# Input transfers of the first layer become tasks of their own, and TensorE multiplies zeros at the start

## The chip, the cores and the metric

One core of a Trainium2 chip runs the whole program. The metric is device time in microseconds (us) of one execution, the median of several runs. A core has five engines that run their own instruction queues in order and wait for each other by semaphores: TensorE (PE; its weight loads are listed as PEld), VectorE (DVE), ScalarE (ACT), GpSimd (POOL) and SyncE (SP). In this kernel SP issues almost every transfer from HBM.

## The reference, cut to what matters

Two layers of a hybrid encoder, 256 tokens of width 2048. Per layer:

```python
h = rms_norm(x, norm_g)
u = h @ w_in                       # 2048 x 15944, cut into q, k, v, z, gates of four branches
mkv = mem @ w_mem_kv               # 256 memory tokens, 2048 x 1024: keys and values of branch M
y = [sparse attention, retention, gated recurrence, attention on mkv]
merged = sum(sigmoid(gate[n]) * ((y[n] * silu(z[n])) @ w_branch[n]) for n in range(4))
x = x + merged @ w_out
```

`mem` doesn't depend on the layers, so the memory keys and values of both layers can be computed first.

## The kernel before, in words

Every large product is done with split operands: a weight tile `raw` in float32 is cast by ACT to `whi` (line 231), DVE subtracts to get `wlo` (line 232), and TensorE adds three matmuls: `whi` by the high part of the activations (line 257), `wlo` by the high part (258) and `whi` by the low part (259).

Weights come in **slabs** of 512 rows of the contraction, 1 MB at the usual 512 columns. A slab is cut into two **half slabs** of 256 rows, each with one `whi` and one `wlo` tile and 12 matmuls of 512 columns. `plan` lists the slabs in order: 16 for the memory keys and values (`mk`, `mv`; two layers, two products, four slabs each), then those of the layers (`u`, `bw`, `wo`). There are four `raw` buffers, and four buffers each for `whi` and `wlo`, so ACT and DVE can be at most four half slabs ahead of TensorE. A load into a `raw` buffer is issued by `split_weights` right behind the second cut of the oldest slab, and SP waits for DVE to be done with that buffer.

Side work is written as Python generators. `stream.add` makes one a **task**. After each half slab's matmuls `gemms` calls `stream.pump()`, which counts a tick and lets at most two tasks take a step, and then `split_weights()`. So a step's instructions stand, on each engine, between the cuts of two half slabs. A bare `yield` in a task passes to a later tick; `stream.rest(n)` blocks it for n ticks. Nothing is reordered behind this: what an engine meets in its queue is what was written first.

`constants()` (line 640) is one task. It loads a first block of constants (`csb`), `qks`, `ngs` and `lbs`, then four blocks of the transposed input (`xr`, from `xt`), each followed two yields later by `split_scaled` (lines 282 and 283), which cuts `xr` into `x0bh` and `x0bl`. Then four blocks of `x` into `xs`, each followed two yields later by two squares on ACT (line 661), then the scale `rs`, the rest of the constants, and masks on POOL. While it is the first task in the list it takes a step at each tick. Its result is asked for behind the memory products, by `stream.finish(start)`.

`fold` transposes a tile by 32x32 blocks: one DVE transpose and 16 small transfers, on POOL and SP in turn (line 308). The memory keys of layer 0 pass through one (`mk0pt`), and ACT scales the result (line 360).

Of the kernel before, what the change touches and what calls it, by code (L numbers as in the profile page):

```python
# [13 lines left out]
AF = mybir.ActivationFunctionType  # L14
# [69 lines left out]
BLOCKED = object()  # L84
# [2 lines left out]
    ((0, 0), (0, 1), (0, 2), (0, 3), (1, 0), (1, 1), (1, 2), (1, 3)),  # L87
)
GEN, HL, RAW = 18, 4, 4
MOVES, STEPS, BANKS = 4, 2, 2  # L90


class Stream:
# [79 lines left out]
def trunk(ctx: ExitStack, tc: tile.TileContext, x, xt, memt, ng, qkg, hg, lbl, win, wmem, wbr, wout,  # L173
          cf, out):
    nc = tc.nc
    te, ve, ac, po, sy = nc.tensor, nc.vector, nc.scalar, nc.gpsimd, nc.sync
# [4 lines left out]
    xtp = ctx.enter_context(tc.tile_pool(name="xtp", bufs=8))  # L181
# [4 lines left out]
    def G(shape, name, dt=F32):  # L186
        return gen.tile(shape, dt, tag="g", name=name)

    def SM(n, name):
        return sml.tile([128, n], F32, tag="s", name=name)  # L190

    def PB(name):
        return psb.tile([128, 1024], F32, tag="pb", name=name)

    def dram(t, off, pitch, n):
        return bass.AP(tensor=t.tensor, offset=t.offset + off, ap=[[pitch, 128], [1, n]])

    xs = cst.tile([128, 2, DM], F32, name="xs")
    csb = cst.tile([128, C_END], F32, name="csb")
    msb = cst.tile([128, len(LEVELS) * 512], U8, name="msb")  # L200
    ngs = cst.tile([128, L, 16], F32, name="ngs")
# [8 lines left out]
    stream = Stream()  # L210

    def load(fine=False):
        src, off, n = plan[stream.loaded]
        raw = wpool.tile([128, 4, n], F32, tag="raw", name="raw", bufs=RAW)
        stream.loaded += 1
        stream.raw.append((raw, n))

        def part(a, b):
            sy.dma_start(raw[:, a:b, :].rearrange("p k n -> p (k n)"), dram(src, off + a * n, 4 * n, (b - a) * n))
        if fine:  # L220
            return part
        part(0, 4)

    def split_weights(fine=False):
        raw, n = stream.raw[0]
        j = stream.cut % 2
        hi = wpool.tile([128, 2, n], F32R, tag="hi", name="whi")
        lo = wpool.tile([128, 2, n], F32R, tag="lo", name="wlo")
        for a, b in [(0, 1), (1, 2)] if fine else [(0, 2)]:
            r = raw[:, 2 * j + a:2 * j + b, :]  # L230
            ac.copy(hi[:, a:b, :], r)  # L231
            ve.tensor_sub(lo[:, a:b, :], r, hi[:, a:b, :].bitcast(F32))  # L232
        stream.parts.append((hi, lo))
        stream.cut += 1
        if j:
            stream.raw.popleft()
            if stream.loaded < len(plan):
                load()
# [32 lines left out]
    def split(src, pool, tag, name):  # L271
        hi = pool.tile([128, 4, 256], F32R, tag=tag, name=name + "h")
        lo = pool.tile([128, 4, 256], F32R, tag=tag, name=name + "l")
        ac.copy(hi, src)
        ve.tensor_sub(lo, src, hi.bitcast(F32))
        return hi, lo

    def split_scaled(src, g, pool, tag, name):
        hi = pool.tile([128, 4, 256], F32R, tag=tag, name=name + "h")
        lo = pool.tile([128, 4, 256], F32R, tag=tag, name=name + "l")  # L280
        for k in range(4):
            ac.activation(hi[:, k, :], src[:, k, :], AF.Copy, scale=g[:, k:k + 1])
            ve.scalar_tensor_tensor(lo[:, k, :], src[:, k, :], g[:, k:k + 1], hi.bitcast(F32)[:, k, :],
                                    op0=OP.mult, op1=OP.subtract)
        return hi, lo

    def rsq(ss, n, scale, name):
        v = SM(n, name + "v")
        ve.tensor_scalar(v, ss, scale, EPS, op0=OP.mult, op1=OP.add)
        r = SM(n, name + "r")  # L290
        po.tensor_tensor(r, v, nhalf.to_broadcast([128, n]), op=OP.pow)
        return r
# [309 lines left out]
    def split_pieces(hi, lo, raw, cuts):  # L602
        for k0, k1 in cuts:
            ac.copy(hi[:, k0:k1, :], raw[:, k0:k1, :])
            ve.tensor_sub(lo[:, k0:k1, :], raw[:, k0:k1, :], hi[:, k0:k1, :].bitcast(F32))

    def split_later(raw, after, name):
        yield from stream.rest(after)
        return split(raw, gen, "g", name)

    part = load(True)
    part(0, 1)
    raw = G([128, 4, 256], "memr")
# [10 lines left out]
        sy.dma_start(memr[b], memt[:, 4 * b:4 * b + 4, :])  # L624
    hi = G([128, 4, 256], "memh", F32R)
    lo = G([128, 4, 256], "meml", F32R)
    split_pieces(hi, lo, raw, [(0, 1), (1, 2)])
    split_weights(True)
    split_pieces(hi, lo, raw, [(2, 4)])
    split_weights(True)  # L630
    split_weights()
    split_weights()
# [4 lines left out]
    def keep(key, steps):  # L637
        box[key] = yield from steps

    def constants():  # L640
        sy.dma_start(csb[:, :C_D], cf[:, :C_D])
        sy.dma_start(qks, qkg)
        yield
        sy.dma_start(ngs, ng)
        sy.dma_start(lbs, lbl)
        yield
        xh = []
        for b in range(4):
            raw = G([128, 4, 256], "xr")
            sy.dma_start(raw, xt[:, 4 * b:4 * b + 4, :])  # L650
            yield
            yield
            xh.append(split_scaled(raw, ngs[:, 0, 4 * b:4 * b + 4], xtp, "xt", f"x0{b}"))
        ssq = SM(8, "ssq0")
        for c in range(4):
            sy.dma_start(xs[:, :, c * 512:c * 512 + 512], x[:, :, c * 512:c * 512 + 512])
            yield
            yield
            for t in range(2):
                sq = G([128, 512], "xsq")  # L660
                ac.activation(sq, xs[:, t, c * 512:c * 512 + 512], AF.Square,
                              accum_out=ssq[:, t * 4 + c:t * 4 + c + 1])
        rs = rms(ssq, 0)
        sy.dma_start(csb[:, C_D:], cf[:, C_D:])
        for i in range(len(LEVELS)):
            po.tensor_copy(msb[:, 512 * i:512 * i + 512].rearrange("p (g t) -> p g t", g=8),
                           csb[:, C_LEV + 64 * i:C_LEV + 64 * i + 64][:, None, :].to_broadcast([128, 8, 64]))
        lower_bounds()
        return xh, rs

    lbv = cst.tile([128, L, NH], F32, name="lbv")
    olb = cst.tile([128, L, NH], F32, name="olb")
# [1 line left out]
    def lower_bounds():  # L674
        mx, e, sm = SM(4, "lbm"), SM(8, "lbe").rearrange("p (l h) -> p l h", l=2), SM(4, "lbsum")
        ve.tensor_max(mx, lbs[:, 0, :], lbs[:, 1, :])
        for l in range(L):
            ve.tensor_sub(e[:, l, :], lbs[:, l, :], mx)
        ac.activation(e, e, AF.Exp)
        ve.tensor_add(sm, e[:, 0, :], e[:, 1, :])  # L680
        ve.reciprocal(sm, sm)
        for l in range(L):
            ve.tensor_mul(e[:, l, :], e[:, l, :], sm)
        ve.tensor_sub(lbv[:, 0, :], e[:, 0, :], e[:, 0, :])
        ve.tensor_add(sm, e[:, 0, :], e[:, 1, :])
        ve.tensor_sub(lbv[:, 1, :], sm, e[:, 0, :])
        ve.tensor_scalar(olb, lbv, -1.0, 1.0, op0=OP.mult, op1=OP.add)

    def rms(ssq, l):
        s2 = SM(2, f"ss{l}")  # L690
        ve.reduce_sum(s2, ssq.rearrange("p (t c) -> p t c", t=2), axis=AX.X)
        return rsq(s2, 2, 1.0 / DM, f"rs{l}")

    start = stream.add(constants())
    for l in range(L):
        def keys_of(ps, l=l):
            stream.add(keep(f"mk{l}", normed_t(ps, None, qks[:, l, 3:4], f"mk{l}")))

        def values_of(ps, l=l):
# [1 line left out]

        gemms(memx, [(wmem, (2 * l + i) * DM * 512) for i in range(2)], 512, ["mk", "mv"], order=MEM_ORDER[l],
              then=[keys_of, values_of])
    xh, rs = stream.finish(start)

    for l in range(L):
        sy.dma_start(hgs.rearrange("p a b -> p (a b)"), hg[l].partition_broadcast(128))
# [22 lines left out]
        if isinstance(rs, Task):  # L730
            rs = stream.finish(rs)
# [67 lines left out]
                ac.activation(sq, xc[:, t, :], AF.Square, accum_out=nssq[:, t * 4 + c:t * 4 + c + 1])  # L799
            return r  # L800

        def scale_of(nssq, ready):
            while not all(t.done for t in ready):
                yield BLOCKED
            return rms(nssq, 1)

        if l + 1 < L:
            nssq = SM(8, "ssq1")
        nx = []
# [7 lines left out]
            if l + 1 < L:  # L817
                nx.append(stream.add(turned(c, xs[:, :, c * 512:c * 512 + 512], nssq)))
        if l + 1 < L:
            xh, rs = nx, stream.add(scale_of(nssq, list(nx)))  # L820


def _cols(w, chunks):
# [41 lines left out]
```

## Time and profile before

| | us |
|---|---|
| median of 3 runs | 1905.28 (1904.95 to 1905.65) |
| the profiled execution, its own time | 1905.74 |
| span of the profiled execution, first to last instruction | 1903.9 |
| TensorE busy | 1885.3 |
| TensorE's waits on other engines, all named ones | 14.1 |
| mean granted TensorE clock | 0.997 |

The span is what the trace shows; the execution's own time is 1.8 us longer. In rows of the timeline the columns are: start in us from the span's start, length in us, engine, line, operation, output<-input, sizes, count, and in brackets the idle time ahead of it and what ended that. The length of a matmul is modelled and overlaps the next; their rate is read from start to start. In rows of waits: engine, tile and line that waited, what for, us in total, times, the longest. In rows of windows: busy time and instruction count of each engine in a stretch, then the granted TensorE clock, the busy share of the 16 DMA engines and GB/s.

### The profile page before, as it was taken

What the parts mean: (1) busy time and instruction counts of PE and PEld (TensorE: products, weight loads), DVE (VectorE), ACT (ScalarE), POOL (GpSimd) and SP (SyncE); (2) the same over time, 40 slices, a digit from 0 to 9 for tenths busy, and PEclk for the clock granted to TensorE, in tenths of its full rate; (3) what the DMA queues carried; (4) which work ended last, traced back from release to release, by engine and by line L of the source; (5) the groups of instructions that cost most, each with busy time, mean ns of one, the idle gap of its engine ahead of it and who ended that gap; (6) DMA issues with size and microseconds to landing.
All of it is one profiled execution on the core that took longest, in us unless ns stands there. A gap on an engine that the chain in (4) does not pass through costs nothing.

```text
span 1903.9 us, 23024 instructions
## 1 busy us (share of the span) xinstructions
PE 1885.3 (99%) x8736; PEld 1574.5 (83%) x8736; DVE 1127.7 (59%) x1204; ACT 863.5 (45%) x995; POOL 238.7 (13%) x377
## 2 busy tenths in 40 slices
PE   7999999999999999999999999999999999999999
PEld 6788988888888888888888898888888888888887
DVE  5455667776655555455565576767565555555554
ACT  5554345544444444444454435554444444444442
POOL 0211041222200000000000104122220000000000
PEclk9999999999999999999999999999999999999999
DMA  8765566668656565565565557666775656556553
GB/s 311 237 226 178 184 184 197 210 199 206 199 197 210 192 196 199 199 203 186 202 189 214 169 176 209 192 215 187 212 199 199 200 190 208 199 185 204 197 203 107
DMA packets 155502, 379.21 MB, mean 199 GB/s; under 512 B 102528, under 2 KB 103424, under 8 KB 114432
## 3 DMA queue, kind: packets, MB, share of 16 engines
q1 hardware_dynamic: 144128, 366.84, 59.2%
q0 software_dynamic: 11264, 10.90, 2.7%
q8 instruction: 69, 1.13, 0.3%
q14 instruction: 41, 0.34, 0.1%
HBM read 353.82 MB, written 2.10 MB: 187 GB/s over the span
## 4 chain that ended last, share of the span: by engine, by line
PE 94%; DVE 0%; issue 0%; DVEq 0%
PE u L257 24%; PE u L258 24%; PE u L259 24%; PE wo L258 3%; PE wo L259 3%; PE bw L258 3%; PE bw L259 3%; PE bw L257 3%; PE wo L257 3%; PE cl L575 1%; PE mov L439 0%; PE mlg L409 0%; PE ixrp L474 0%; PE aov L439 0%; PE alg L409 0%; PE cdg L562 0%
## 5 line engine op out<-in xcount | busy, mean ns | idle before, releaser
L232 DVE TENSOR_TENSOR wlo<-raw,whi 128x1024 fp32r<-128x1024 f32 (+2 forms) x674 | 802.3, 1197 | 657.7 <-ACT whi L231 657.3
L231 ACT CAST whi<-raw 128x1024 fp32r<-128x1024 f32 (+2 forms) x674 | 693.5, 1033 | 917.6 <-PE u L259 721.8
L308 POOL DMA_DIRECT2D mgp<-mgpi x48 | 27.6, 582 | 588.7 <-ACT whi L231 293.3
L257 PE MATMUL u<-whi,x12h 128*128 128x512 f32 (+2 forms) x256 | 99.0, 387 | 0.0
L257 PE MATMUL u<-whi,x02h 128*128 128x512 f32 (+2 forms) x256 | 99.0, 387 | 0.0
L257 PE MATMUL u<-whi,x11h 128*128 128x512 f32 (+2 forms) x256 | 98.9, 386 | 0.0
L257 PE MATMUL u<-whi,x13h 128*128 128x512 f32 (+2 forms) x256 | 98.9, 386 | 0.0
L257 PE MATMUL u<-whi,x03h 128*128 128x512 f32 (+2 forms) x256 | 98.9, 386 | 0.0
L257 PE MATMUL u<-whi,x01h 128*128 128x512 f32 (+2 forms) x256 | 98.8, 386 | 0.0
L257 PE MATMUL u<-whi,x00h 128*128 128x512 f32 (+2 forms) x256 | 98.4, 384 | 0.0
L257 PE MATMUL u<-whi,x10h 128*128 128x512 f32 (+2 forms) x256 | 98.4, 384 | 0.0
L258 PE MATMUL u<-wlo,x02h 128*128 128x512 f32 (+2 forms) x256 | 98.2, 383 | 0.0
L258 PE MATMUL u<-wlo,x12h 128*128 128x512 f32 (+2 forms) x256 | 98.2, 383 | 0.0
L258 PE MATMUL u<-wlo,x11h 128*128 128x512 f32 (+2 forms) x256 | 98.2, 383 | 0.0
L259 PE MATMUL u<-whi,x11l 128*128 128x512 f32 (+2 forms) x256 | 98.2, 383 | 0.0
L258 PE MATMUL u<-wlo,x03h 128*128 128x512 f32 (+2 forms) x256 | 98.2, 383 | 0.0
L258 PE MATMUL u<-wlo,x13h 128*128 128x512 f32 (+2 forms) x256 | 98.2, 383 | 0.0
L259 PE MATMUL u<-whi,x12l 128*128 128x512 f32 (+2 forms) x256 | 98.2, 383 | 0.0
L259 PE MATMUL u<-whi,x02l 128*128 128x512 f32 (+2 forms) x256 | 98.2, 383 | 0.0
L258 PE MATMUL u<-wlo,x01h 128*128 128x512 f32 (+2 forms) x256 | 98.2, 383 | 0.0
L259 PE MATMUL u<-whi,x01l 128*128 128x512 f32 (+2 forms) x256 | 98.1, 383 | 0.0
L259 PE MATMUL u<-whi,x10l 128*128 128x512 f32 (+2 forms) x256 | 98.1, 383 | 0.0
(370 smaller groups left out, 3706.8 us busy)
## 6 DMA issues: line engine op xcount, KB each, us to landing
raw<-in_win SPq DMA_DIRECT2D x240, 1024.0 KB, 4.9
raw<-in_wbr SPq DMA_DIRECT2D x32, 1024.0 KB, 4.8
raw<-in_wout SPq DMA_DIRECT2D x32, 1024.0 KB, 4.8
raw<-in_wmem SPq DMA_DIRECT2D x15, 1024.0 KB, 7.5
raw<-in_win SPq DMA_DIRECT2D x8, 656.0 KB, 4.2
raw<-in_win SPq DMA_DIRECT2D x8, 512.0 KB, 3.6
xr<-in_xt SPq DMA_DIRECT2D x4, 512.0 KB, 7.5
xs<-in_x SPq DMA_DIRECT2D x4, 512.0 KB, 6.2
```

Of the source, the lines that this page charges most:

```text
L231: ac.copy(hi[:, a:b, :], r)
L232: ve.tensor_sub(lo[:, a:b, :], r, hi[:, a:b, :].bitcast(F32))
L257: te.matmul(ps[:, t, :n], ah[:, 2 * j + k, c], wh[:, k, :], start=first, stop=False)
L258: te.matmul(ps[:, t, :n], ah[:, 2 * j + k, c], wl[:, k, :], start=False, stop=False)
L259: te.matmul(ps[:, t, :n], al[:, 2 * j + k, c], wh[:, k, :], start=False, stop=last)
L308: q.dma_start(whole[b, :, a], inner[a, :, b])
L575: te.matmul(ps[:, g * 64:g * 64 + 64].rearrange("p (b j) -> p b j", j=m), kd[:, g // 2, c], qd[:, g // 2, c].rearrange("p (b two j) -> p b ...
```

## The change

The task `constants()` is split into several. `first_constants` loads the small tiles; `first_turned(b)`, four tasks, issues its `xr` block at tick 3 + 4b and cuts it seven ticks later; `first_squares(c)`, four tasks, issues its block of `x` at tick 19 + 2c and squares it seven ticks later; `last_constants` issues the rest of the constants at tick 27 and uses them seven ticks later. `xh` and `rs` are now tasks that the first product of layer 0 asks for, instead of `stream.finish(start)`.

At the program's head DVE sets a tile `warm` to zero and TensorE does five float32 matmuls of 256 columns on it, into a PSUM tile `heat` that nothing reads. And the first two cuts of the memory input (`split_pieces`) now stand behind the first cut of the weights, instead of ahead of it.

```diff
-MOVES, STEPS, BANKS = 4, 2, 2
+MOVES, STEPS, BANKS, WARM = 4, 2, 2, 5
...
-    def split_weights(fine=False):
+    def split_weights(fine=False, then=None):
...
             ve.tensor_sub(lo[:, a:b, :], r, hi[:, a:b, :].bitcast(F32))
+            if then and a == 0:
+                then()
...
+    warm = G([128, 256], "warm")
+    ve.memset(warm, 0.0)
+    heat = PB("heat")
+    for i in range(WARM):
+        te.matmul(heat[:, :256], warm[:, :128], warm, start=True, stop=True)
     part = load(True)
...
-    split_pieces(hi, lo, raw, [(0, 1), (1, 2)])
-    split_weights(True)
+    split_weights(True, lambda: split_pieces(hi, lo, raw, [(0, 1), (1, 2)]))
...
-    def constants():
-        sy.dma_start(csb[:, :C_D], cf[:, :C_D])
+    def first_constants():
+        yield from stream.rest(1)
+        sy.dma_start(ngs, ng)
+        sy.dma_start(csb[:, :C_D], cf[:, :C_D])
+        yield from stream.rest(2)
         sy.dma_start(qks, qkg)
-        yield
-        sy.dma_start(ngs, ng)
         sy.dma_start(lbs, lbl)
-        yield
-        xh = []
-        for b in range(4):
-            raw = G([128, 4, 256], "xr")
-            sy.dma_start(raw, xt[:, 4 * b:4 * b + 4, :])
-            yield
-            yield
-            xh.append(split_scaled(raw, ngs[:, 0, 4 * b:4 * b + 4], xtp, "xt", f"x0{b}"))
...
+    def first_turned(b):
+        yield from stream.rest(3 + 4 * b)
+        raw = G([128, 4, 256], "xr")
+        sy.dma_start(raw, xt[:, 4 * b:4 * b + 4, :])
+        yield from stream.rest(7)
+        return split_scaled(raw, ngs[:, 0, 4 * b:4 * b + 4], xtp, "xt", f"x0{b}")
...
+    def first_squares(c):
+        yield from stream.rest(19 + 2 * c)
+        sy.dma_start(xs[:, :, c * 512:c * 512 + 512], x[:, :, c * 512:c * 512 + 512])
+        yield from stream.rest(7)
+        for t in range(2):
...
+    def last_constants():
+        yield from stream.rest(27)
         sy.dma_start(csb[:, C_D:], cf[:, C_D:])
+        yield from stream.rest(7)
...
-    start = stream.add(constants())
+    stream.add(first_constants())
+    xh = [stream.add(first_turned(b)) for b in range(4)]
+    rs = stream.add(scale_of(ssq0, [stream.add(first_squares(c)) for c in range(4)], 0))
+    stream.add(last_constants())
...
-    xh, rs = stream.finish(start)
```

ACT before, from the cut of the third half slab on (`memh` is the cut of a block of the memory input):

```order
L231 CAST whi<-raw 128x1024 x3
L274 CAST memh<-memr 128x1024
L231 CAST whi<-raw 128x1024 x3
L274 CAST memh<-memr 128x1024
L282 ACTIVATE x00h<-xr,ngs 128x256 x4
L231 CAST whi<-raw 128x1024 x2
L282 ACTIVATE x01h<-xr,ngs 128x256 x4
```

ACT with the change, the same place (its lines are numbered by the changed file: 276 is 274 before, 284 is 282):

```order
L231 CAST whi<-raw 128x1024 x3
L276 CAST memh<-memr 128x1024
L231 CAST whi<-raw 128x1024 x3
L276 CAST memh<-memr 128x1024
L231 CAST whi<-raw 128x1024 x3
L276 CAST memh<-memr 128x1024
L231 CAST whi<-raw 128x1024 x3
L284 ACTIVATE x00h<-xr,ngs 128x256 x4
L231 CAST whi<-raw 128x1024 x2
L339 COPY mk0u<-mk 128x512 x2
```

The first cut of the input stood ahead of the half slabs 9 to 14 and stands behind them now; six casts of weights have moved past it.

SP before, from the first load of the transposed input on:

```order
L650 DMA xr<-in_xt 128x1024
L219 DMA raw<-in_wmem 128x2048
L650 DMA xr<-in_xt 128x1024
L219 DMA raw<-in_wmem 128x2048
L650 DMA xr<-in_xt 128x1024
L219 DMA raw<-in_wmem 128x2048
L650 DMA xr<-in_xt 128x1024
L219 DMA raw<-in_wmem 128x2048
L656 DMA xs<-in_x 128x2x512
```

SP with the change, from the same load on:

```order
L657 DMA xr<-in_xt 128x1024
L219 DMA raw<-in_wmem 128x2048 x2
L657 DMA xr<-in_xt 128x1024
L219 DMA raw<-in_wmem 128x2048 x2
L657 DMA xr<-in_xt 128x1024
L219 DMA raw<-in_wmem 128x2048 x2
L657 DMA xr<-in_xt 128x1024
L219 DMA raw<-in_wmem 128x2048
L310 DMA mk0pt<-mk0pti 32x8x32 x2
```

Between two loads of the input there are now two loads of weights instead of one, and the loads of `xs` have moved behind the first moves of the memory keys.

TensorE's head with the change; before, its first row was the `mk` matmul:

```order
L617 MATMUL heat<-warm 128x256 x5
L259 MATMUL mk<-whi,memh 128x512
L260 MATMUL mk<-wlo,memh 128x512
L261 MATMUL mk<-whi,meml 128x512
L259 MATMUL mk<-whi,memh 128x512
```

Apart from these five, TensorE's instructions and their order are those of before.

## Rows read from the trace of the kernel before

**Rows 1.** The profile page: busy time and share of the span, by engine.
```profile
PE 1885.3 (99%) x8736; PEld 1574.5 (83%) x8736; DVE 1127.7 (59%) x1204; ACT 863.5 (45%) x995; POOL 238.7 (13%) x377
```
**Rows 2.** Waits of TensorE over the whole span.
```profile
PE mk L257 <- ACT whi L231: 10.5, 3, 5.5
PE mk L258 <- DVE wlo L232: 3.0, 4, 1.0
PE mv L258 <- DVE wlo L232: 0.6, 1, 0.6
```
**Rows 3.** Timeline of TensorE from its first matmul on.
```profile
5.52 0.80 PE L257 MATMUL mk<-whi,memh 128*128 128x512 f32 x1 [5.52 <-ACT whi L231]
...
11.03 0.40 PE L257 MATMUL mk<-whi,memh 128*128 128x512 f32 x1
...
14.31 0.50 PE L258 MATMUL mv<-wlo,memh 128*128 128x512 f32 x1
```
**Rows 4.** Timeline of ACT and DVE ahead of 14.31 us.
```profile
11.94 2.00 ACT L231 CAST whi<-raw 128x1024 fp32r<-128x1024 f32 x2 [1.89 <-DMA raw<-in_wmem]
...
8.99 0.69 DVE L232 TENSOR_TENSOR wlo<-raw,whi 128x512 fp32r<-128x512 f32 x1
10.09 0.69 DVE L232 TENSOR_TENSOR wlo<-raw,whi 128x512 fp32r<-128x512 f32 x1 [0.40 <-ACT whi L231]
13.03 2.36 DVE L232 TENSOR_TENSOR wlo<-raw,whi 128x1024 fp32r<-128x1024 f32 x2 [2.25 <-ACT whi L231]
```
**Rows 5.** Timeline of TensorE around the end of the fourth slab.
```profile
30.32 0.39 PE L259 MATMUL mv<-whi,meml 128*128 128x512 f32 x1
34.04 0.50 PE L257 MATMUL mk<-whi,memh 128*128 128x512 f32 x1 [3.33 <-ACT whi L231]
35.30 0.80 PE L258 MATMUL mk<-wlo,memh 128*128 128x512 f32 x1 [0.76 <-DVE wlo L232]
...
38.36 0.39 PE L259 MATMUL mk<-whi,meml 128*128 128x512 f32 x1
```
**Rows 6.** Timeline of SP's queue and ACT around the first cut of the input.
```profile
20.75 0.43 SPq L650 DMA_DIRECT2D xr<-in_xt  x1
...
31.35 1.70 ACT L282 ACTIVATE x00h<-xr,ngs 128x256 fp32r<-128x256 f32 x4 [9.47 <-DMA xr<-in_xt]
32.96 1.98 ACT L231 CAST whi<-raw 128x1024 fp32r<-128x1024 f32 x2
```
**Rows 7.** Two windows of the first 32 us.
```profile
0.00:20.00 20.00, 14.36 (x50) 11.04 (x51) 9.76 (x13) 11.08 (x15) 0.20 (x4) 1.00 0.88 325
20.00:32.00 12.00, 10.71 (x48) 8.54 (x46) 3.86 (x5) 2.53 (x4) 0.00 (x0) 1.00 1.02 407
```
**Rows 8.** Timeline of TensorE around 80 us.
```profile
76.61 0.39 PE L259 MATMUL mk<-whi,meml 128*128 128x512 f32 x1
78.61 0.50 PE L257 MATMUL mk<-whi,memh 128*128 128x512 f32 x1 [1.61 <-ACT whi L231]
80.09 0.80 PE L258 MATMUL mk<-wlo,memh 128*128 128x512 f32 x1 [0.98 <-DVE wlo L232]
...
86.14 0.39 PE L257 MATMUL mk<-whi,memh 128*128 128x512 f32 x1
```
**Rows 9.** Timeline of ACT ahead of that.
```profile
75.28 0.63 ACT L661 ACTIVATE xsq<-xs 128x512 f32<-128x512 f32 x1 [4.17 <-DMA xs<-in_x]
...
77.53 3.87 ACT L231 CAST whi<-raw 128x1024 fp32r<-128x1024 f32 x4
```
**Rows 10.** Timeline of TensorE: a later half slab's first matmul, and the first of the layers.
```profile
58.30 0.39 PE L257 MATMUL mk<-whi,memh 128*128 128x512 f32 x1
...
110.89 0.39 PE L257 MATMUL u<-whi,x00h 128*128 128x512 f32 x1
```
**Rows 11.** Waits of ACT, the first 115 us.
```profile
ACT mk0pt L360 <- DMA mk0pt<-mk0pti: 6.5, 1, 6.5
```
**Rows 12.** The chain that ended last: four float32 matmuls of 256 columns.
```profile
389.14 1.73 PE alg L409 x8
```

More of the change, by code (lines that the diff above doesn't have):

```diff
@@ L638, in keep @@
         box[key] = yield from steps
-    def constants():
+    def first_constants():
+        yield from stream.rest(1)
+        sy.dma_start(ngs, ng)
         sy.dma_start(csb[:, :C_D], cf[:, :C_D])
+        yield from stream.rest(2)
         sy.dma_start(qks, qkg)
-        yield
-        sy.dma_start(ngs, ng)
         sy.dma_start(lbs, lbl)
-        yield
-        xh = []
-        for b in range(4):
-            raw = G([128, 4, 256], "xr")
-            sy.dma_start(raw, xt[:, 4 * b:4 * b + 4, :])
-            yield
-            yield
-            xh.append(split_scaled(raw, ngs[:, 0, 4 * b:4 * b + 4], xtp, "xt", f"x0{b}"))
[L654 to L663, printed above, removed]
+    def first_turned(b):
[4 more added lines that the diff above has]
+        return split_scaled(raw, ngs[:, 0, 4 * b:4 * b + 4], xtp, "xt", f"x0{b}")
+    ssq0 = SM(8, "ssq0")
+    def first_squares(c):
[3 more added lines that the diff above has]
+        for t in range(2):
+            sq = G([128, 512], "xsq")
+            ac.activation(sq, xs[:, t, c * 512:c * 512 + 512], AF.Square,
+                          accum_out=ssq0[:, t * 4 + c:t * 4 + c + 1])
+    def last_constants():
+        yield from stream.rest(27)
         sy.dma_start(csb[:, C_D:], cf[:, C_D:])
+        yield from stream.rest(7)
         for i in range(len(LEVELS)):
@@ L668, in constants @@
         lower_bounds()
-        return xh, rs
     lbv = cst.tile([128, L, NH], F32, name="lbv")
@@ L692, in rms, with scale_of @@
         return rsq(s2, 2, 1.0 / DM, f"rs{l}")
-    start = stream.add(constants())
+    def scale_of(ssq, ready, l):
+        while not all(t.done for t in ready):
+            yield BLOCKED
+        return rms(ssq, l)
+    stream.add(first_constants())
+    xh = [stream.add(first_turned(b)) for b in range(4)]
+    rs = stream.add(scale_of(ssq0, [stream.add(first_squares(c)) for c in range(4)], 0))
+    stream.add(last_constants())
     for l in range(L):
@@ L800, in turned @@
             return r
[L802 to L805, printed above, removed]
         if l + 1 < L:
@@ L819, in trunk @@
         if l + 1 < L:
-            xh, rs = nx, stream.add(scale_of(nssq, list(nx)))
+            xh, rs = nx, stream.add(scale_of(nssq, list(nx), 1))
 def _cols(w, chunks):
```

## The prediction

> **What bounds the kernel now.** I read the page's engine lines first: TensorE is busy 1885.3 us [rows 1], so all that can be won without taking matmuls away lies in its idle time and in stretches at the lower clock. Next I read whom it waits for, over the whole span [rows 2]: every named wait is on a matmul of `mk` or `mv`, none on one of `u`, `bw` or `wo`. The reader is to see that the whole loss lies in the memory products, ahead of the first `u` matmul at 110.89 us [rows 10]; behind it TensorE never waits, and the change leaves its order there alone. So the question is by how much the first `u` matmul moves.
>
> The rate: from 38.36 us [rows 5] to 58.30 us [rows 10] TensorE does 88 matmuls without a wait (from the 9th of the fifth slab to the first of the ninth), 19.94 / 88 = 0.2266 us from start to start. A half slab of 12 is 2.72 us.
>
> Then the timeline, for the three long losses.
>
> *The head, to 14.31 us.* The first matmul starts at 5.52 us and the 13th at 11.03 us [rows 3]: 0.46 us each, half the rate. But what ends this stretch is a wait: the matmul at 14.31 us needs the first `wlo` of the second slab, which DVE makes from 13.03 us on (two in 2.36 us, so the first at about 14.2), behind a cast that ACT began at 11.94 us after 1.89 us of waiting for the transfer [rows 4].
>
> *Around 30 us.* The fourth slab ends at 30.32 + 0.23 = 30.55 us. The next matmul comes at 34.04 us, the one after it at 35.30 us, and matmuls at 0.2266 us are back only at 38.36 us [rows 5]; eight started in 7.81 us instead of 1.81, so 6.00 us are lost. ACT shows why: it idles 9.47 us for `xr`, issued at 20.75 us and landed at 31.35 us, and the cast that TensorE needs stands right behind, at 32.96 us [rows 6].
>
> *Around 80 us.* The same with `xs`: ACT idles 4.17 us in front of the last squares, and four casts in a row follow at 77.53 us [rows 9]. TensorE is out of work at 76.61 + 0.23 = 76.84 us and back at the full rate at 86.14 us, 15 matmuls in 9.30 us instead of 3.40 [rows 8]: 5.90 us lost.
>
> What is left are short waits of about 0.9 us for `wlo` [rows 2].
>
> **The change part by part.**
>
> *Input and squares as tasks.* Seven half slabs between issue and use are 7 x 2.72 = 19.0 us. The slowest input transfer that I see took 31.35 - 20.75 = 10.6 us [rows 6], in the stretch where the DMA engines are full. So ACT meets these cuts with 8 us to spare, and its waits on `xr` and `xs` go. What is late next must be looked at. The weights of the fifth slab: what SP issues up to their end is four slabs, the four blocks of the memory input (2 MB) and their own 1 MB, 7 x 1.05 = 7.3 MB. At 325 GB/s the first 20 us bring 6.5 MB, and the rest comes at 407 GB/s [rows 7] by 22 us; with two or three us until ACT sees it, 25 us. Their cut needs 1.05 us on ACT and 1.2 on DVE, and TensorE wants it at 30.55 us: 3 us to spare. From there on a load has 19 us from its issue to its cut too, for 1 MB every 5.4 us, under 200 GB/s against the 407 that were reached. Buffers let ACT run four half slabs, 10.9 us, ahead of TensorE. With the lead kept, a delay on ACT or DVE below 10.9 - 2.3 (cast and subtraction) = 8.6 us doesn't reach TensorE. The waits for `wlo` of 0.9 us each came behind the two long stalls, when the lead was gone; I count them as won. The small tiles, the masks on POOL and the bounds on DVE are moved behind tick 34, that is in the first `u` products; they cost ACT and DVE what they cost before, under the same lead. On POOL the scale and the masks now queue behind the moves of layer 1's memory keys; the scale is wanted only behind the first `u` product, eight half slabs or 21.8 us after the memory products, and it is written before their end. So TensorE runs from 30.55 us without a wait: slabs five to sixteen are 288 matmuls, 288 x 0.2266 = 65.3 us, first `u` matmul at 95.8 us. Before it was 110.89 us: **15.1 us won** (6.0 + 5.9 + 3.2 for the short waits).
>
> *The zeros.* Five matmuls of 256 float32 columns. The trace has four such in 1.73 us at the full rate [rows 12], so five are 2.2 us, and at half rate 4.3 us. The memset isn't shown; it lies between nothing and a 0.69 us DVE instruction of 512 columns [rows 4], in a stretch where DVE has no data. The zeros end between 3 and 6 us, so the first real matmul lies within 0.5 us of 5.52 either way. Does the clock buy anything? If every real matmul runs at 0.2266 us, the first slab waits for its pieces: the third piece's `wlo` is done at 8.99 + 0.69 = 9.68 us, its last five matmuls end at 10.8, the fourth's (`wlo` at 10.78) at 12.2 us [rows 4]. Then TensorE waits for the same transfer as before and does the matmul of 14.31 us at 14.31 us. The zeros move the idle time behind the first slab: I cost them at 0, hidden by the transfer of the second slab. Were that cover gone, they would give 5.51 us for 12 matmuls [rows 3] less 12 x 0.2266, 2.8 us.
>
> [...]
>
> *The cuts at the head* change places within ACT's first 2 us of work: ACT is done with them ahead of the transfer that it waits for at 11.94 us. 0.
>
> *Sum.* The profiled execution took 1905.74 us; 1905.74 - 15.1 = 1890.6. The median of the runs is 0.46 us lower, so I say **1890.2 us**.
>
> **The rivals.**
>
> *The head wins too.* Were the second slab there in time, 1890.2 - 2.8 = 1887.4 us. For it: half the rate in 5.5 us of the head. Against: ACT's 1.89 us of waiting for that slab's transfer, which nothing here makes earlier. 6 in 100.
>
> *The clock falls in the new gap.* Between 12.2 and 14.31 us TensorE has one matmul to do. At 76.84 us, 3.25 us with one matmul left it at half rate [rows 8]; the waits of up to 1 us that stand alone [rows 2] did not. Ours lies between. The two cases cost (35.30 to 38.36, seven matmuls) 1.5 us and (80.09 to 86.14, fourteen) 2.9 us [rows 5, 8], so 1891.7 to 1893.1 us. 10 in 100.
>
> *A wait is left.* ACT still meets the transposed memory keys in its queue, where it idled 6.5 us before [rows 11], and the chain of key norms on DVE and POOL is as it was. One short wait costs 0.9 us, one that lets the clock fall 5.9 us: 1891.1 to 1896.1 us. Against: 8.6 us of lead. 10 in 100.
>
> *Nothing gained.* If the transfers themselves, and not ACT's waiting for them, held the weights back at 30 and 76 us, the stalls stay: 1905 us. For it: full DMA engines to 32 us [rows 7]. Against: right behind the cut of `xr` ACT did its casts without a wait [rows 6]; the weights had landed. 4 in 100.
>
> *Slower.* The moves of the memory keys now share SP's queue with more loads in flight, and ACT waits for all of them in one instruction, the next casts behind it. It decides where that wait is longer than the lead: each us above 8.6 is lost, and to end 3.8 us above 1905.3 it must be 8.6 + 15.1 + 3.8 = 27.5 us, four times the 6.5 of before: 1909 us. 3 in 100.
>
> **How the numbers follow.** The forecast has 67 in 100, with its own range of 1889 to 1891.5 us. A measurement of this kernel can tell about 0.2%, 3.8 us, from no change. Faster by more are the forecast, the first three rivals: 0.93; same 0.04; slower 0.03. The range from 1888.0 to 1894.0 us holds the forecast, the fallen clock and half of the case with a wait left: 82 in 100.
>
> **What would show it.** Right: no wait of ACT on `xr` or `xs`, the first `u` matmul at 95 to 97 us, no TensorE wait between 14.5 us and there, the granted clock full from the head on, and still a wait for `wlo` near 14.3 us. Wrong: a matmul of the second slab well ahead of 14 us (the head wins), half the rate behind 14.3 us (the clock fell), a long ACT wait at `mk0pt`.

## The result and the profile after

The changed kernel takes 1891.85 us (median of 4 runs, 1890.96 to 1892.38); the kernel before, run beside it, 1905.47 us (1904.95 to 1905.88). The ratio is 0.9928 with a 95% interval of 0.9911 to 0.9945: faster by 13.6 us. The time is 1.7 us above the forecast of 1890.2 us, inside the range of 1888.0 to 1894.0 us, and 0.4 us above the narrower 1889 to 1891.5 us that the forecast had for itself. The profiled execution took 1891.51 us with a span of 1889.7 us.

The page's engine line, to be read against [rows 1]: TensorE has ten instructions more (the five zero matmuls are two each) and its idle time has fallen from 18.6 to 7.9 us.

```profile
PE 1881.8 (100%) x8746; PEld 1573.3 (83%) x8746; DVE 1129.4 (60%) x1205; ACT 865.2 (46%) x995; POOL 239.7 (13%) x377
```

The waits of TensorE over the whole span, as [rows 2] (engine, tile and line, what for, us in total, times, the longest):

```profile
PE heat L617 <- DVE warm L614: 1.2, 1, 1.2
PE mv L260 <- DVE wlo L232: 0.8, 1, 0.8
PE mv L259 <- ACT whi L231: 0.5, 1, 0.5
PE mk L259 <- ACT whi L231: 0.5, 1, 0.5
PE mk L260 <- DVE wlo L232: 0.4, 2, 0.2
```

All five lie in the first 15.2 us. Both long stalls are gone, and so are the three short waits that stood alone (0.60 to 0.65 us of idle time, at 65, 71 and 106 us). TensorE's timeline at the places of [rows 3, 10] (start, length, engine, line, operation, and the idle time ahead with its releaser; 259 to 261 are 257 to 259 of before):

```profile
1.23 4.55 PE L617 MATMUL heat<-warm 128*128 128x256 f32 x10 [1.23 <-DVE warm L614]
5.30 0.70 PE L259 MATMUL mk<-whi,memh 128*128 128x512 f32 x1
5.84 0.40 PE L260 MATMUL mk<-wlo,memh 128*128 128x512 f32 x1
...
13.01 0.39 PE L261 MATMUL mk<-whi,meml 128*128 128x512 f32 x1
13.94 0.50 PE L259 MATMUL mv<-whi,memh 128*128 128x512 f32 x1 [0.55 <-ACT whi L231]
15.20 0.51 PE L260 MATMUL mv<-wlo,memh 128*128 128x512 f32 x1 [0.76 <-DVE wlo L232]
...
96.69 0.39 PE L259 MATMUL u<-whi,x00h 128*128 128x512 f32 x1
```

The zeros did what they were made for: from 5.84 us on real matmuls run at the full rate, 0.23 us from start to start where nothing is waited for. And it bought nothing: the matmul that waited for the second slab's first `wlo` stands at 15.20 us, 0.9 us later than before [rows 3]. The chain that ended last, from 0 to 20 us (start, us, what), says what it hangs on:

```profile
3.98 0.04 issue
4.02 8.80 DMA raw<-in_wmem
```

That is the transfer of the second slab: 8.80 us from issue to landing. ACT, as [rows 4, 6]:

```profile
12.84 2.00 ACT L231 CAST whi<-raw 128x1024 fp32r<-128x1024 f32 x2 [1.89 <-DMA raw<-in_wmem]
...
24.20 1.05 ACT L231 CAST whi<-raw 128x1024 fp32r<-128x1024 f32 x1 [1.46 <-DMA raw<-in_wmem]
...
38.01 1.71 ACT L284 ACTIVATE x00h<-xr,ngs 128x256 fp32r<-128x256 f32 x4
```

The fifth slab is cast at 24.20 us, where it stood behind the input until 32.96 us before [rows 6], and the first cut of the input begins without a wait. For the readings below I use one number: the first `u` matmul less the start of the second slab's first cast. Here it is 96.69 - 12.84 = 83.85 us, which is what TensorE needs when it has no stop behind the wait at 15.20 us that this cast ends. Before it was 110.89 - 11.94 = 98.95 us [rows 4, 10], 15.1 us more. That excess is the **loss** of a run behind its head. It is read from one trace each, and where a stall waits for the input and not for the second slab it shifts with that slab's landing, by about 1 us (15.1 and 14.0 us in the two traces with the old tasks).

### The profile page after: what moved, and what is told of

Same layout as the page of the kernel before. It is cut to its first block, busy times and chain, and to the rows that moved or that the text cites. A ratio compares the mean times of both kernels' runs of the same rounds, so it can differ in the third digit from the quotient of the medians.

```text
span 1889.7 us, 23051 instructions
## 1 busy us (share of the span) xinstructions
PE 1881.8 (100%) x8746; PEld 1573.3 (83%) x8746; DVE 1129.4 (60%) x1205; ACT 865.2 (46%) x995; POOL 239.7 (13%) x377
## 4 chain that ended last, share of the span: by engine, by line
PE 99%; DMA 0%; SPq 0%; DVE 0%; ACT 0%; DVEq 0%; issue 0%
PE u L259 24%; PE u L261 24%; PE u L260 24%; PE wo L259 3%; PE bw L259 3%; PE wo L261 3%; PE wo L260 3%; PE bw L261 3%; PE bw L260 3%; PE cl L577 1%; PE mv L260 1%; PE mv L261 1%; PE mv L259 1%; PE mk L261 1%; PE mk L260 1%; PE mk L259 1%
```

## The experiments

Each was timed beside runs of the kernel before on the same chip (medians 1905.2, 1904.87 and 1905.45 us for the three groups of four).

**The tasks alone.** The zeros taken out, the first cuts as before.

```diff
-    warm = G([128, 256], "warm")
-    ve.memset(warm, 0.0)
-    heat = PB("heat")
-    for i in range(WARM):
-        te.matmul(heat[:, :256], warm[:, :128], warm, start=True, stop=True)
...
-    split_weights(True, lambda: split_pieces(hi, lo, raw, [(0, 1), (1, 2)]))
+    split_pieces(hi, lo, raw, [(0, 1), (1, 2)])
+    split_weights(True)
```

> The tasks alone: no zeros, and the first cuts in the order of before. Theory (the gain is that ACT no longer waits for the input's transfers; the zeros are worth nothing, since the second slab's transfer ends the head): no TensorE wait between 16 and 95 us, the first u matmul at 96 to 97 us, 1891 to 1892.5 us, the same as the change. Rival (the zeros give part of the gain, up to 2.8 us): 1893.5 to 1895 us, the first u matmul at 98 to 99.5 us.

1891.67 us, ratio 0.9929 (0.9916 to 0.9941): the whole gain. TensorE's timeline:

```profile
5.54 0.79 PE L259 MATMUL mk<-whi,memh 128*128 128x512 f32 x1 [5.54 <-ACT whi L231]
...
15.14 0.49 PE L260 MATMUL mv<-wlo,memh 128*128 128x512 f32 x1 [0.76 <-DVE wlo L232]
...
96.67 0.39 PE L259 MATMUL u<-whi,x00h 128*128 128x512 f32 x1
```

The first slab starts at half rate (0.43 us from start to start between 6.86 and 9.42 us) and ends with the same wait at the same place. The second slab's cast began at 12.78 us, so the loss is 96.67 - 12.78 - 83.85 = 0.0 us.

**The zeros alone.** The kernel before with the zeros and the new order of the first cuts.

```diff
+    for i in range(WARM):
+        te.matmul(heat[:, :256], warm[:, :128], warm, start=True, stop=True)
     part = load(True)
...
-    split_pieces(hi, lo, raw, [(0, 1), (1, 2)])
-    split_weights(True)
+    split_weights(True, lambda: split_pieces(hi, lo, raw, [(0, 1), (1, 2)]))
```

> The zeros and the new order of the first cuts alone, with the one task of before. Theory: the wait for the second slab's first wlo stays near 14.3 to 15.2 us, both long stalls stay, 1904.5 to 1906.5 us. Rival (the zeros win the head): that matmul before 13 us, 1902 to 1903 us. A third reading, that the zeros or the new order make the first pieces land later: the matmul at 15.2 us as in the change, and later pieces than in the run without zeros.

1906.23 us, ratio 1.0005 (0.9996 to 1.0014): no change. The second slab's cast began at 12.93 us, 0.15 us later than in the run without zeros, which is little beside the spread between runs (11.73 to 13.24 us, below) and gives the third reading no support. The first `u` matmul came at 110.77 us. TensorE's timeline:

```profile
15.28 0.50 PE L260 MATMUL mv<-wlo,memh 128*128 128x512 f32 x1 [0.76 <-DVE wlo L232]
...
33.65 0.77 PE L259 MATMUL mk<-whi,memh 128*128 128x512 f32 x1 [1.98 <-ACT whi L231]
...
94.78 0.50 PE L259 MATMUL mv<-whi,memh 128*128 128x512 f32 x1 [1.77 <-ACT whi L231]
96.04 0.50 PE L260 MATMUL mv<-wlo,memh 128*128 128x512 f32 x1 [0.76 <-DVE wlo L232]
96.38 0.40 PE L261 MATMUL mv<-whi,meml 128*128 128x512 f32 x1
```

The wait for the second slab stays, at 15.28 us. Together the two runs settle that the zeros win nothing here; the first of them shows it by time and this one by that wait, since a gain at the head could be eaten by the stalls behind it. One part of my expectation missed: the stall near 30 us stays (5.9 us lost), but near 78 us only 1.9 us go, and 3.1 us go near 95 us instead, behind ACT's wait of 9.4 us for the turned memory keys. The loss is 110.77 - 12.93 - 83.85 = 14.0 us, with the same tasks that lost 15.1 us in the trace of before.

**Two ticks for the input.** The rest of seven ticks ahead of `split_scaled` becomes two; the blocks are still four ticks apart.

```diff
         sy.dma_start(raw, xt[:, 4 * b:4 * b + 4, :])
-        yield from stream.rest(7)
+        yield from stream.rest(2)
```

> The change, but each block of the transposed input is cut two ticks after its issue instead of seven. Theory (ACT's wait for a landing of some 10 us, with the casts queued behind it, made the stall at 30 us): ACT waits 5 to 9 us for the first block, TensorE stalls near 30 us again, 6 us lost, 1897 to 1899 us. Rival (the stalls come from the number of transfers in flight, or the distance is of no matter): 1891 to 1892.5 us.

1893.2 us, ratio 0.9943 (0.9929 to 0.9958), 0.7 us outside the rival's range too. My expectation fell: ACT does wait, TensorE hardly does. ACT's waits of the first 115 us:

```profile
ACT mk0pt L362 <- DMA xs<-in_x: 6.1, 1, 6.1
ACT x00h L284 <- DMA xr<-in_xt: 5.8, 1, 5.8
...
ACT x03h L284 <- DMA xr<-in_xt: 4.5, 1, 4.5
...
ACT x01h L284 <- DMA xr<-in_xt: 3.7, 1, 3.7
...
ACT x02h L284 <- DMA xr<-in_xt: 2.4, 1, 2.4
```

That is 16.4 us on `xr`, more than the 13.9 us of the kernel before (9.5 + 3.0 + 1.4), and the loss is 97.78 - 11.81 - 83.85 = 2.1 us instead of 15.1. The trace is of an execution of 1892.97 us; two of the five took 1896.1 and 1896.3 us, and what they lost beyond it no trace shows. The timeline near 30 us shows why the stall stays away, on ACT and on TensorE:

```profile
23.16 1.05 ACT L231 CAST whi<-raw 128x1024 fp32r<-128x1024 f32 x1 [1.41 <-DMA raw<-in_wmem]
30.04 1.71 ACT L284 ACTIVATE x00h<-xr,ngs 128x256 fp32r<-128x256 f32 x4 [5.83 <-DMA xr<-in_xt]
31.65 1.99 ACT L231 CAST whi<-raw 128x1024 fp32r<-128x1024 f32 x2
...
34.01 0.50 PE L260 MATMUL mk<-wlo,memh 128*128 128x512 f32 x1 [0.48 <-DVE wlo L232]
```

The first step of a task falls into tick 1, so a rest of 3 and a rest of 2 put the cut at tick 6, where the old task had it at tick 5. By that one half slab the cast of the ninth half slab (23.16 us) stands ahead of the waiting cut and not behind it. TensorE has 2.7 us more of work, and when that runs out it waits 0.48 us.

**Two ticks for the squares.**

```diff
         sy.dma_start(xs[:, :, c * 512:c * 512 + 512], x[:, :, c * 512:c * 512 + 512])
-        yield from stream.rest(7)
+        yield from stream.rest(2)
```

> The change, but each block of x is squared two ticks after its issue instead of seven. Reading A (the waits on xs made the stall near 80 us by themselves): ACT waits 3 to 5 us in front of squares and TensorE loses about 6 us, 1897 to 1898 us. Reading B (the lead of four half slabs had been lost in the stall at 30 us, and with the lead whole a wait of 5 us doesn't reach TensorE): ACT waits, TensorE doesn't, 1891 to 1892.5 us.

1891.41 us, ratio 0.9926 (0.9913 to 0.9939): reading B. Of ACT's waits:

```profile
ACT xsq L669 <- DMA xs<-in_x: 4.0, 3, 1.9
```

The loss is 96.57 - 12.66 - 83.85 = 0.1 us. With its lead whole ACT meets the blocks 3.4 to 7.7 us after their issue, 5.4 us on average, and waits up to 1.9 us, which TensorE doesn't feel. Before, with the lead lost at 30 us, ACT met them 1.6 to 5.4 us after their issue, 3.6 us on average, and waited 11.6 us in all, up to 4.7. I read it so, without a run of its own: an engine that is behind catches up on its queue, so issue and use come closer in time than their distance in half slabs says.

**The second slab not loaded.** Its cuts read the first slab's tile; 1 MB of transfer and the first slab of `mv` are left out. Once with the zeros, once without.

```diff
     def load(fine=False):
         src, off, n = plan[stream.loaded]
+        if stream.loaded == 1:
+            stream.loaded += 1
+            stream.raw.append(stream.raw[0])
+            return
```

> The change, but the second slab is never loaded: its cuts read the first slab's raw tile, so 1 MB of transfer in the head is left out (the values of mv's first slab are then those of mk). This takes away what I say ends the head. Theory (the second slab's transfer ends the head): no TensorE wait of 0.5 us or more behind the first slab, the first slab done at 12 to 13.3 us, the first u matmul 360 x 0.2266 = 81.6 us later, at 93.8 to 94.9 us; about 1889 to 1890 us. Rival (the cuts on ACT and DVE end the head, not the transfer): the first u matmul at 96 us or later, 1891 us or more.

> As the kernel with the shared first slab (1 MB of transfer left out in the same way), but without the zeros. With the cover gone the zeros should have a price: the first slab then runs partly at half rate and ends at 13.6 to 14.2 us, the first u matmul at 95.2 to 95.8 us, 0.6 to 1.9 us later than with the zeros. Rival (the zeros are worth nothing even so, because the first slab's pieces arrive no faster than half rate takes): the same first u matmul within 0.3 us.

1890.58 us with the zeros, 1891.28 us without; the profiled executions have the first `u` matmul at 95.28 and at 97.34 us. TensorE's timeline with the zeros:

```profile
10.34 0.51 PE L263 MATMUL mk<-whi,memh 128*128 128x512 f32 x1 [0.95 <-ACT whi L235]
11.07 0.50 PE L264 MATMUL mk<-wlo,memh 128*128 128x512 f32 x1 [0.22 <-DVE wlo L236]
...
13.68 0.39 PE L263 MATMUL mv<-whi,memh 128*128 128x512 f32 x1
13.90 0.39 PE L264 MATMUL mv<-wlo,memh 128*128 128x512 f32 x1
```

The wait at the second slab is gone, which confirms that its transfer made it, but the start misses my range by 0.4 us: the third piece of the first slab was cast at 9.67 us only, and the first slab itself ended at 13.7 us. Without the zeros:

```profile
9.12 0.39 PE L265 MATMUL mk<-whi,meml 128*128 128x512 f32 x1
10.79 0.50 PE L263 MATMUL mk<-whi,memh 128*128 128x512 f32 x1 [1.28 <-ACT whi L235]
11.52 0.65 PE L264 MATMUL mk<-wlo,memh 128*128 128x512 f32 x1 [0.22 <-DVE wlo L236]
11.96 0.63 PE L265 MATMUL mk<-whi,meml 128*128 128x512 f32 x1
```

The full rate came at about 8.1 us and was lost in the wait for the third piece; eight matmuls from 11.52 us on take 0.43 us each. So with the cover gone the zeros are worth 97.34 - 95.28 = 2.1 us in these two traces, of which 0.45 us is a third piece that landed later without them. But the trace without zeros is of the slowest of its five executions (1892.51 us), and the medians differ by 0.7 us, with intervals that overlap (0.9909 to 0.9936 with the zeros, 0.9916 to 0.9941 without). That the zeros have a price is seen in the traces; its size is not settled.

**Second and third slab in halves.** Meant to beat the change: the second slab's first half can be cut before its second half lands.

```diff
-        part(0, 4)
+        if stream.loaded in (2, 3):
+            part(0, 2)
+            part(2, 4)
+        else:
+            part(0, 4)
```

> The change, with the second and the third slab loaded in two halves each, so that the cut of the first half needn't wait for the second. Theory (the head ends when the second slab's transfer does): the second slab's first cut begins 1.0 to 1.3 us sooner against the landing, its first wlo is there near 14.0 us instead of 15.2, the first u matmul at 95.2 to 95.9 us, 1890.3 to 1891.0 us. Rival (a transfer more costs as much as it frees, or the third slab then waits): 1891.5 to 1892.5 us. The landings of the first pieces have differed by 0.9 us between runs, so I read the first u matmul against the second slab's landing.

1891.46 us, ratio 0.9928 (0.9916 to 0.9940): no change. The wait for the second slab fell to 0.25 us, at 14.68 us, and TensorE waited 1.48 us for the third piece of the first slab instead; the first `u` matmul came at 96.19 us, 0.3 us outside what I expected.

**One half slab later.** The kernel before with one `yield` more.

```diff
         sy.dma_start(lbs, lbl)
         yield
+        yield
         xh = []
```

> The kernel before, with one more yield ahead of the first input block, so that every step of the one task stands one half slab later and nothing else changes. Reading A (TensorE stalled near 30 us because the waiting cut stood ahead of the one cast that it needed next; one half slab later, 2.7 us of work and a shorter wait cover most of it): the stall near 30 us falls from 6.0 to 0.5 to 2 us, and the one near 80 us with it or not, 1893 to 1901 us. Reading B (the two-tick rhythm of issue and use is what stalls, wherever it stands): the stalls stay within 1 us, 1904 to 1906 us.

1900.67 us, ratio 0.9978 (0.9969 to 0.9987). Reading A holds for the stall near 30 us: one word removes it, though in this trace the second slab's cast began 1.3 us later than before (13.24 us), which also moved TensorE's need back. In two runs of this set whose first cut stands behind that cast as well and whose second slab came early (11.81 and 11.73 us), TensorE waits there 0.48 and 0.57 us, so the landing isn't the reason. TensorE's timeline:

```profile
35.20 0.50 PE L258 MATMUL mk<-wlo,memh 128*128 128x512 f32 x1 [0.27 <-DVE wlo L232]
...
73.58 0.50 PE L257 MATMUL mk<-whi,memh 128*128 128x512 f32 x1 [0.20 <-ACT whi L231]
75.04 0.50 PE L258 MATMUL mk<-wlo,memh 128*128 128x512 f32 x1 [0.96 <-DVE wlo L232]
89.01 0.50 PE L257 MATMUL mv<-whi,memh 128*128 128x512 f32 x1 [3.02 <-ACT whi L231]
90.27 0.79 PE L258 MATMUL mv<-wlo,memh 128*128 128x512 f32 x1 [0.76 <-DVE wlo L232]
```

The loss is 105.31 - 13.24 - 83.85 = 8.2 us. What is left is another wait of ACT:

```profile
86.88 1.15 ACT L360 ACTIVATE mk0pt<-mk0pt,qks 128x1024 f32<-128x1024 f32 x1 [10.51 <-DMA mk0pt<-mk0pti]
```

It is the place of my slower rival: 10.5 us of waiting for the turned memory keys, against the 8.6 us that I gave the lead. TensorE is then idle for 3.0 and 0.8 us and goes on at half rate (its matmuls at 92.57 and 93.00 us are still 0.43 us apart).

**The old rhythm as tasks.** Input blocks two ticks apart and cut two ticks after issue; squares as in the change.

```diff
-        yield from stream.rest(3 + 4 * b)
+        yield from stream.rest(3 + 2 * b)
         raw = G([128, 4, 256], "xr")
         sy.dma_start(raw, xt[:, 4 * b:4 * b + 4, :])
-        yield from stream.rest(7)
+        yield from stream.rest(2)
```

> The change, but the input blocks are issued two ticks apart and cut two ticks after issue, the rhythm of the kernel before, one half slab later than there; the squares keep their seven ticks. Reading A (the first cut's place decides; the lead then covers the rest): TensorE waits under 1.5 us in all between 16 and 95 us, 1891.5 to 1894 us. Reading C (four such waits of ACT within 25 us use the lead up, and a stall of several us comes behind them): 1895 to 1900 us.

1895.03 us, ratio 0.9944 (0.9931 to 0.9958): at the edge of reading C by time, but no stall of several us. TensorE's waits of this run:

```profile
PE mv L260 <- DVE wlo L232: 1.8, 3, 0.8
...
PE mk L260 <- DVE wlo L232: 1.2, 2, 0.6
PE mv L259 <- ACT whi L231: 1.0, 2, 0.5
```

Apart from those in the head there are short waits at 34, 48, 49, 61 and 94 us; the loss is 99.84 - 11.73 - 83.85 = 4.3 us. Both readings were too coarse: the lead is eaten and won back several times.

**Fewer, wider transfers in the head**, alone and with the two slabs in halves.

```diff
-    part(0, 1)
-    raw = G([128, 4, 256], "memr")
-    for k0, k1 in [(0, 1), (1, 2), (2, 4)]:
-        sy.dma_start(raw[:, k0:k1, :], memt[:, k0:k1, :])
-        for k in range(max(k0, 1), k1):
-            part(k, k + 1)
+    part(0, 2)
+    raw = G([128, 4, 256], "memr")
+    sy.dma_start(raw, memt[:, 0:4, :])
+    part(2, 4)
...
-    split_weights(True, lambda: split_pieces(hi, lo, raw, [(0, 1), (1, 2)]))
-    split_pieces(hi, lo, raw, [(2, 4)])
-    split_weights(True)
+    split_weights()
+    split_pieces(hi, lo, raw, [(0, 2), (2, 4)])
+    split_weights()
```

> The change, with the head's transfers in three instead of seven: the first slab in two halves, the first block of the memory input whole between them, cut in halves. Theory (the head is bound by how fast the first 1.5 MB and the second slab land, and the small pieces go at some 200 to 250 GB/s where whole slabs go at over 400): the first real matmul later, at 6.5 to 7.5 us, the second slab's first cast at 10.3 to 11.3 us instead of 11.9 to 12.8, the first u matmul at 94.5 to 95.8 us, 1889.5 to 1890.8 us. Rival (the later start costs what the rate gives, or the clock falls in the gap behind the zeros): first u matmul at 96 us or later, 1891.5 us or more.

> As the kernel with three wide transfers in the head, and the second and third slab in two halves each. Theory: both together take the wait for the second slab away, TensorE runs from its first real matmul on, the first u matmul at 93.8 to 95 us, 1889 to 1890.3 us. Rival: as before, 1891.5 us or more.

1891.69 and 1891.54 us, ratios 0.9926 (0.9914 to 0.9939) and 0.9927 (0.9915 to 0.9940): no better than the change, as the rival said. The transfers came sooner (320 GB/s from 4 to 6 us and 387 from 6 to 8 in the first of them, 230 and 274 in the change once more, below), the second slab's cast began at 11.04 us in that run, but its TensorE timeline shows what that was given back for:

```profile
7.29 0.50 PE L259 MATMUL mk<-whi,memh 128*128 128x512 f32 x1 [1.81 <-ACT memh L606]
...
8.34 0.79 PE L261 MATMUL mk<-whi,meml 128*128 128x512 f32 x1
...
11.48 0.54 PE L259 MATMUL mk<-whi,memh 128*128 128x512 f32 x1
```

Behind the zeros TensorE waited 1.81 us, and from 8.34 to 11.48 us it ran at half rate (0.43 us from start to start from 8.92 us on, granted clock 0.59 from 8 to 10 us). Longer zeros to bridge that wait were not tried.

**The change once more**, beside these.

> The change once more, beside the versions that try to beat it: 1891 to 1892.5 us. The second slab's first cast begins at 11.8 to 12.9 us; if it is 11.9 us as in the kernel before, the first u matmul comes at 95.8 us, so that the 0.9 us by which I was off is the landing of the first transfers in one run or another; if it is 12.7 us or more again, the zeros or the new order have a part in it.

1891.38 us, ratio 0.9925 (0.9912 to 0.9937). The second slab's cast began at 13.06 us, the first `u` matmul at 96.92 us, so 83.86 us again. By what I had written ahead of it, so late a cast speaks for a part of the zeros or the new order in it; the nine traces compared below don't bear that out. No version tried beats the change by more than the intervals.

## Why the prediction was right, and what was off

*The bound and the place.* Right: nothing outside the memory products changed, and the first `u` matmul carries the result: 110.89 - 96.69 = 14.2 us, the spans differ by 14.2 us, the profiled executions by 1905.74 - 1891.51 = 14.2 us.

*The sum, 15.1 us.* The losses of 6.0, 5.9 and 3.2 us are gone in full: no wait of TensorE is left behind 15.2 us. (The 3.2 us was what the subtraction left over; the three short waits make 2.4 of it by their starts, and none was as long as the 0.9 us that I gave them.) What was mis-sized is the head, where I wrote that TensorE "does the matmul of 14.31 us at 14.31 us"; it did it at 15.20 us, 0.9 us later, because the second slab landed later. The change is not the cause: with SP issuing at the same times, this cast began at 11.94, 12.78 and 13.24 us in the three runs without zeros and with that slab loaded whole through the same pieces, and at 12.84, 12.93, 11.81, 12.66, 11.73 and 13.06 us in the six with zeros: 12.65 and 12.51 us on average. I had anchored the sum on one early landing. The other 0.8 us lie between profiled executions and medians: I subtracted 0.46 us because the one of before was that much above its median, and the one of after was 0.34 us below its own.

*Where the 15.1 us came from.* Here the reason I gave was only partly right. I put the gain down to the 19.0 us between issue and use (for the first block 15.4 us in the change, from 22.59 to 38.01 us). The runs take it apart by the losses: 15.1 us before; 8.2 with everything one half slab later; 4.3 when the squares and the bounds go to their new places as well, and ACT's long wait for the memory keys with them; 2.1 when the input blocks are four ticks apart; none with seven ticks from issue to use. The medians, each against the kernel before beside it, give the same steps as 4.2, 6.2, 1.6 and 1.6 us. Neither of the last two steps is clear of noise by itself: the two runs that make the third have ratios of 0.9944 and 0.9943. So the distance itself seems worth some 2 us for the input, and nothing for the squares. The one cast that no longer stands behind the first waiting cut is worth 4 to 7 us, the step with the squares and the memory keys 4 to 6; which is larger, and how the second divides, these runs leave open. I had named that cast in reading the stall, and then priced the wait and not its place. That the sum held all the same is in part luck: it needed only that every wait behind the head go, whatever part of the change took it away.

*The stall near 80 us.* I took it to be made by the squares' waits. With the lead kept the same two-tick distance costs nothing, so those waits alone don't make it; the lead lost at 30 us has its part. What then comes down there isn't fixed: with the zeros alone it was 1.9 us, after the same stall at 30 us. One more thing stood there that I had not priced. In the kernel before, the scale and the lower bounds (`lower_bounds`) come between the last squares and the next casts, and both ACT and DVE pass through them:

```profile
77.41 0.21 ACT L679 ACTIVATE lbe<-lbe 128x8 f32<-128x8 f32 x1 [0.79 <-DVE lbe L678]
...
78.81 4.63 DVE L232 TENSOR_TENSOR wlo<-raw,whi 128x1024 fp32r<-128x1024 f32 x4
```

ACT was done with the squares at 76.5 us and began the casts at 77.53 us. The change moves the bounds too, and no run moves them alone, so some 1 us of the 5.9 may be theirs. The short waits, which I did put down to the lost lead, went with it as I had said.

*The zeros at 0.* Right, by both runs, and for the reason given: the transfer covers them. The price with the cover gone was forecast at 2.8 us and came to 2.1 us in the traces and 0.7 us in the medians. The trace shows what the zeros give, the full rate from 5.84 us on, where the run of the tasks alone has it from 9.69 us on, and the time doesn't follow, as the transfer ends the head.

*The rivals.* The fallen clock did not happen in the change's gap (13.24 to 15.20 us with one matmul, full rate and a granted clock of 1.00 behind it), but it did in three variants (the second slab not loaded, without zeros: granted clock 0.91 over the first 20 us; both with wider transfers: 0.59 and 0.50 from 8 to 10 us), so 10 in 100 was not too much. The other case from which I priced it, 3.25 us with one matmul [rows 8], is no rule either: with the zeros alone a gap of 3.19 us with one matmul kept the full rate (92.85 to 96.04 us). The weights had landed in time: the fifth slab was cast at 24.20 us, where I worked out 25. The two or three us until ACT sees a load were my estimate, with no row behind it; here 7.35 MB, the 7.3 that I counted up to the slab's end, had moved by 22.0 us (334 GB/s), and the cast came 2.2 us after that. The slower rival's mechanism showed in the run with one `yield` more, at a TensorE wait of 3.0 us, and in that of the zeros alone, at 1.8 us, both times with the lead gone before.

## What to carry to other kernels

In an in-order queue a wait costs by what stands behind it and by the lead that the engine has there, not by its length: 16.4 us of waits for the input went with a loss of 2.1 us of TensorE time, and with 13.9 us of them, the first ahead of one cast that was needed, TensorE lost 6.0 us at once and 15.1 us by the end. So look first at which instruction the starving engine needs next and whether it can stand ahead of the wait; with the lead lost the later waits were longer too (11.6 us for the squares, 4.0 us with it whole). And don't hang a forecast within 1 us on one execution's landing times at a program's start.

## What the hardware showed that I had not expected

The landing of the first transfers spreads: with issue times alike, the second slab's first cast began between 11.73 and 13.24 us in nine profiled runs. And the gaps that leave TensorE at half rate are not told by their length alone: an idle 1.81 us behind the zeros, and a wait from 9.35 to 11.52 us with one matmul in it, did so (0.43 us from start to start); 13.24 to 15.20 us with one matmul in it did not, nor did 92.85 to 96.04 us with the zeros alone. The way up differs as much: in the four traces without zeros the full rate came some 3.3, 4.0, 5.3 and 6.0 us after the first matmul, so what a start without them costs is not one number either. In the kernel before, the windows' granted clock reads 1.00 from 6 to 10 us although the matmuls start 0.43 us apart there, as they do from 36 to 38 us and from 81 to 85 us, where it reads 0.50; in that head the rate from start to start is the better witness.
